# Moving every tile of an HGRN2 and forgetting-attention kernel to a rounder start address in SBUF

## The chip, the cores and the metric

The kernel runs on one core of one Trainium2 chip. A core has TensorE (PE in the profile, its weight loads shown apart as PEld), VectorE (DVE), ScalarE (ACT), GpSimd (POOL) and SyncE (SP, which here only issues DMAs). SBUF is the on-chip working memory; a tile in it is a block of bytes at the same address in each of up to 128 partitions. The metric is the device time of one execution in microseconds.

## The reference, cut to what matters

The program computes two residual layers over 512 tokens of width 2048, all float32. Layer one is a gated linear recurrence (HGRN2) with 16 heads of 128, computed in blocks; layer two is attention with a learned forget gate (FoX), 16 heads of 128, whose keys and values come from the stream after layer one.

```python
def hgrn2_layer(x, norm_w, w_in, lb, out_norm_w, w_out):
    h = rmsnorm(x, norm_w)
    proj = h @ w_in                                  # 2048 -> 8192: q, fz, i, gate
    log_f = jnp.logaddexp(jnp.log(lb), jnp.log1p(-lb) + jax.nn.log_sigmoid(fz))
    k = (1.0 - lb) * jax.nn.sigmoid(-fz)
    o = hgrn2_chunkwise(q, k, i, log_f)
    o = head_rmsnorm(o, out_norm_w) * jax.nn.silu(gate)
    return x + o @ w_out

def fox_layer(x, norm_w, w_in, q_norm_w, out_norm_w, w_out, k, v, F):
    proj = rmsnorm(x, norm_w) @ w_in                 # 2048 -> 4096: q, gate
    q = head_rmsnorm(q, q_norm_w)
    o = forgetting_attention(q, k, v, F)             # softmax(q.k/sqrt(d) + F[t] - F[s])
    o = head_rmsnorm(o, out_norm_w) * jax.nn.silu(gate)
    return x + o @ w_out
```

## The kernel before

**Products.** Each float32 operand is held as two float32r tiles, a rounded value (names ending in h) and the remainder (names ending in l), and a product is three matmuls: h·h, h·l and l·h. `group` computes one 512-column slice of a projection: for each of 16 slices of the 2048 inputs it takes a pair `wh`, `wl` of weights and streams tokens against them. Feature-major groups (L227 to L229) use 128-column pieces of `wh`/`wl` as the stationary operand and stream the 512 columns of `xh`/`xl`; token-major groups (L223 to L225, the value projections) do the reverse, with pieces of `xh`/`xl` stationary and `wh`/`wl` streamed. In the profile an operand list `gm<-xh,wh` names the output, then the streamed operand, then the stationary one.

**Feeding it.** SP loads 512 KB of raw weights into one of two `wr` buffers. ACT casts half of it to `wh` (L432, or L137 where a norm weight is multiplied in) and DVE subtracts to get `wl` (L433, L138).

**Stages.** Stage A runs the projections of layer one, with the recurrence of the heads (`mix_a`) pumped in between; an output product follows, its last three quarters by `quick`, a seven-product scheme on 256-column halves (L282 to L284); stage B and a second output product do the same for layer two, with `mix_b` as the heads' work. `attend` (L426 to L428) is the heads' product with the values, `v_evac` (L413) takes the values out of PSUM, `split` (L432, L433) makes an h and l pair.

**Where tiles lie.** Three pools of SBUF tiles stand one behind another: `cp`, made by `const`, holds small constants, the norm weights, the masks of 32 to 128 bytes and the two score tiles `at`; `sb`, through `nt`, holds what lives all through the program (`xh`, `xl`, `y`, `z`, `wr`, `rstd`); and a pool of the stage, through `mt`, opened anew by `phase`, holds the rest (`wh`, `wl`, `t`, `q`, `k`, `v` and so on). In each pool tiles lie one after another, each size rounded up to 32 bytes. So a constant of 4 bytes or a mask of 96 shifts all that comes behind it, and `rstdc`, 16 bytes at the end of `sb`, shifts the stage's pool by 32 bytes against `sb`. The order of the instructions on each engine is made by a scheduler from the program's dependences.

Of the kernel before, what the change touches and what calls it, by code (L numbers as in the profile page):

```python
# [1 line left out]

# [8 lines left out]
U8 = mybir.dt.uint8  # L11
# [4 lines left out]
P = 128  # L16
# [4 lines left out]
NW = 4  # L21
# [10 lines left out]
def hgrn2_fox(ctx, tc, io):  # L32
# [3 lines left out]
    cp = ctx.enter_context(tc.tile_pool(name="cp", bufs=1))  # L36
    sb = ctx.enter_context(tc.tile_pool(name="sb", bufs=1))
# [4 lines left out]
    uid = [0]  # L42

    def nt(tag, shape, bufs, dt=F32, pool=None):
        uid[0] += 1
        return (pool or sb).tile(list(shape), dt, tag=tag, name=f"{tag}_{uid[0]}", bufs=bufs)

    def const(tag, shape, dt=F32):
        return cp.tile(list(shape), dt, tag=tag, name=tag)

    def view(t, offset, dims):
        return bass.AP(t.tensor, t.offset + offset, [t.ap[0], *dims])
# [7 lines left out]
    def bank():  # L60
        return nt("mx", (P, T), 4, pool=ps)

    def mt(tag, shape, bufs=1, dt=F32):

        return nt(tag, shape, bufs, dt, cur["sb"])
# [36 lines left out]


    eps = const("eps", (P, 1))
    G.memset(eps, EPS)
    ones_f = tmp()
    G.memset(ones_f[:, :P], 1.0)
    ones = const("ones", (P, P), F32R)
    V.tensor_copy(ones, ones_f[:, :P])
    ident = const("ident", (P, P))  # L110
    make_identity(nc, ident)

# [45 lines left out]
    class Chunks:  # L158
# [15 lines left out]
        def load(self):  # L174

            if not self.todo:
                return
            ap, quick, scales, kt = self.todo.pop(0)
            r = nt("wr", (P, 2 * T), 2)
            nc.sync.dma_start(r, ap)  # L180
            if quick:
                self.raw.append((lambda r=r.rearrange("p (a b c) -> p a b c", a=2, c=P): w_split_quick(r, w_sums(r)), 2))
            else:
                for i in range(2):
                    self.raw.append((lambda v=r[:, i * T : (i + 1) * T], k=kt + i: [w_split(v, k, scales)], 1))
# [134 lines left out]
    def sum_parts(x, out_bank):  # L320

        half = P // 2
        s = x
        hl = mt("sl", (P, T), 2, F32R)
        V.tensor_add(s[:half], x[:half], x[half:])
        V.tensor_copy(hl[:half], s[:half])
        V.tensor_sub(hl[half:], s[:half], rd(hl)[:half])
        PE.matmul(out_bank, ones, hl, start=True, stop=True)

    def rsqrt_mean(out, sums, n):  # L330
        S.activation(out, sums, AF.Ln, scale=1.0 / n, bias=eps)
        S.activation(out, out, AF.Exp, scale=-0.5)

    class Norm:
# [15 lines left out]
        def finish(self):  # L350
            b = bank()
            sum_parts(self.acc, b)
            self.row = nt("rstd", (P, T), 1)
            rsqrt_mean(self.row, b, D)
            b2 = bank()
            for w in range(NW):
                PE.transpose(b2[:, w * P : (w + 1) * P], self.row[:, w * P : (w + 1) * P], ident)
            self.col = nt("rstdc", (P, NW, 1), 1)
            V.tensor_copy(self.col, b2.rearrange("p (w c) -> p w c", c=P)[:, :, 0:1])


# [720 lines left out]
```

## Time and profile before

| | us |
|---|---|
| median of 3 runs | 2089.97 |
| lowest, highest run | 2087.96, 2094.06 |
| the profiled execution | 2092.97 |
| its span, first to last instruction | 2091.2 |

The profile page has the busy share of each engine, a strip of 40 slices over the span, the chain of work that ended last, and groups of instructions by source line. A group's row gives the line, engine, operation, out<-in by tile names, shape and count, then its busy time, the mean duration of one in ns, and the idle time of the engine before it with what ended it. Matmuls overlap in the pipeline, and so the duration of one (some 396 ns for 512 columns) is not the time it costs: that is the distance between the starts of two in a row, which the timeline gives.

### The profile page before, as it was taken

To read this page: it belongs to the slowest core of one execution; us is meant where nothing else is said; L and a number is where in the kernel's file an instruction comes from. 1 tells how busy PE (TensorE), PEld (TensorE's weight loads), DVE (VectorE), ACT (ScalarE), POOL (GpSimd) and SP (SyncE) were. 2 spreads that over 40 slices of the span, in tenths; PEclk is the share of its full clock that TensorE was granted. 3 is DMA by queue.
4 is the path that set the end of the run, shared out by engine and by line. 5 is a ranking of instruction groups with operands and counts; after the bars stand their busy time and mean duration, and the time that the engine had idled before them with its cause. 6 is when DMAs were issued, how large, how long until landed. Compare 5 with 4: busy or idle time off the path is not lost.

```text
span 2091.2 us, 28900 instructions
## 1 busy us (share of the span) xinstructions
PE 2028.2 (97%) x10202; PEld 1701.7 (81%) x10202; DVE 1579.0 (76%) x3250; ACT 1132.6 (54%) x2312; POOL 316.1 (15%) x404
## 2 busy tenths in 40 slices
PE   7999999999999999988989999999999999999798
PEld 5888888888888888768977888888888888888698
DVE  8778977988799788769884667665766666685887
ACT  5646655666566465634443555554555556564343
POOL 7303210322132031211210000010001000011100
PEclk9999999999999999989999999999999999999899
DMA  5222222222222222233533232223222222223353
GB/s 172 81 81 81 71 81 71 81 81 71 81 71 81 76 76 71 90 117 117 161 104 91 87 95 91 86 78 99 91 86 87 91 91 86 86 82 109 101 165 108
DMA packets 61408, 195.01 MB, mean 93 GB/s; under 512 B 7872, under 2 KB 8000, under 8 KB 61264
## 3 DMA queue, kind: packets, MB, share of 16 engines
q1 hardware_dynamic: 61120, 193.17, 29.5%
q8 instruction: 80, 1.31, 0.3%
q14 instruction: 64, 0.52, 0.1%
q10 hardware_dynamic: 144, 0.01, 0.0%
HBM read 184.73 MB, written 8.42 MB: 92 GB/s over the span
## 4 chain that ended last, share of the span: by engine, by line
PE 83%; DVE 7%; DMA 3%; ACT 2%; issue 2%; POOL 2%; SPq 0%; DVEq 0%; ACTq 0%; POOLq 0%
PE gm L227 17%; PE gm L229 17%; PE gm L228 17%; PE gm L224 5%; PE gm L223 5%; PE gm L225 5%; DVE wl L433 3%; DMA wr<-in_wb_q 2%; PE mx L580 1%; PE mx L579 1%; PE mx L578 1%; PE mx L427 1%; PE mx L428 1%; PE mx L284 1%; PE mx L426 1%
## 5 line engine op out<-in xcount | busy, mean ns | idle before, releaser
L227 PE MATMUL gm<-xh,wh 128*128 128x512 f32 x1664 | 662.0, 398 | 13.9 <-ACT wh L432 8.3
L228 PE MATMUL gm<-xl,wh 128*128 128x512 f32 x1664 | 661.8, 398 | 0.0
L229 PE MATMUL gm<-xh,wl 128*128 128x512 f32 x1664 | 625.6, 398 | 5.7 <-DVE wl L433 5.5
L227 PEld LDWEIGHTS gm<-xh,wh 128*128 128x128 f32 x1664 | 314.3, 189 | 86.5 <-ACT wh L432 8.3
L229 PEld LDWEIGHTS gm<-xh,wl 128*128 128x128 f32 x1664 | 312.1, 189 | 77.6 <-DVE wl L433 7.0
L228 PEld LDWEIGHTS gm<-xl,wh 128*128 128x128 f32 x1664 | 314.5, 189 | 71.6
L432 ACT CAST wh<-wr 128x512 fp32r<-128x512 f32 (+1 forms) x336 | 217.3, 649 | 232.5 <-PE gm L228 125.8
L433 DVE TENSOR_TENSOR wl<-wr,wh 128x512 fp32r<-128x512 f32 (+1 forms) x336 | 261.8, 783 | 107.7 <-ACT wh L432 101.5
L138 DVE SCALAR_TENSOR_TENSOR wl<-wr,v_b_norm_w,wh 128x256 fp32r<-128x256 f32 (+1 forms) x192 | 113.7, 594 | 152.1 <-ACT wh L137 141.2
L137 ACT ACTIVATE wh<-wr,v_b_norm_w 128x256 fp32r<-128x256 f32 (+1 forms) x192 | 111.9, 586 | 196.8 <-PE gm L228 155.9
L224 PE MATMUL gm<-wl,xh 128*128 128x512 f32 x512 | 203.7, 398 | 0.4 <-DVE wl L433 0.4
L225 PE MATMUL gm<-wh,xl 128*128 128x512 f32 x512 | 202.1, 396 | 0.0
L223 PE MATMUL gm<-wh,xh 128*128 128x512 f32 x512 | 185.8, 396 | 0.0
L137 ACT ACTIVATE wh<-wr,v_kv_norm_w 128x256 fp32r<-128x256 f32 (+1 forms) x192 | 110.3, 575 | 63.2 <-PE gm L225 46.2
L138 DVE SCALAR_TENSOR_TENSOR wl<-wr,v_kv_norm_w,wh 128x256 fp32r<-128x256 f32 (+1 forms) x192 | 111.2, 580 | 38.6 <-ACT wh L137 38.0
L924 POOL TENSOR_SCALAR_AFFINE_SELECT s<-s 128x128 f32<-128x128 f32 x64 | 27.4, 428 | 669.7 <-DVE s L923 669.0
L573 DVE COPY_PREDICATED at<-m,mx 128x128 f32<-128x128 uint8 (+3 forms) x448 | 106.6, 296 | 13.6 <-PE mx L580 13.0
L223 PEld LDWEIGHTS gm<-wh,xh 128*128 128x128 f32 x512 | 95.9, 188 | 22.4 <-DVE q L544 0.2
L224 PEld LDWEIGHTS gm<-wl,xh 128*128 128x128 f32 x512 | 96.2, 188 | 21.5 <-DVE wl L433 0.9
L225 PEld LDWEIGHTS gm<-wh,xl 128*128 128x128 f32 x512 | 96.1, 188 | 20.9
L432 ACT CAST kh<-k 128x512 fp32r<-128x512 f32 (+1 forms) x96 | 56.4, 587 | 52.0 <-PE mx L579 25.8
L382 POOL TENSOR_TENSOR z<-z,t 128x512 f32<-128x512 f32 x32 | 47.9, 1509 | 237.0 <-ACT t L381 236.9
(217 smaller groups left out, 3893.9 us busy)
## 6 DMA issues: line engine op xcount, KB each, us to landing
wr<-in_wa_qf SPq DMA_DIRECT2D x64, 512.0 KB, 3.6
wr<-in_wb_qk SPq DMA_DIRECT2D x64, 512.0 KB, 3.5
wr<-in_wa_v SPq DMA_DIRECT2D x32, 512.0 KB, 3.5
wr<-in_wa_g SPq DMA_DIRECT2D x32, 512.0 KB, 3.5
wr<-in_wb_v SPq DMA_DIRECT2D x32, 512.0 KB, 3.5
wr<-in_wb_g SPq DMA_DIRECT2D x32, 512.0 KB, 3.5
wr<-in_wa_q SPq DMA_DIRECT2D x24, 512.0 KB, 3.6
wr<-in_wb_q SPq DMA_DIRECT2D x24, 512.0 KB, 3.6
```

The source lines that it names most:

```text
L137: S.activation(h[:, c], r[:, c], AF.Copy, scale=w[:, kt : kt + 1])
L138: V.scalar_tensor_tensor(l[:, c], r[:, c], w[:, kt : kt + 1], rd(h)[:, c], op0=ALU.mult, op1=ALU.subtract)
L223: PE.matmul(banks[j], xh, h, start=f, stop=False)
L224: PE.matmul(banks[j], xh, l, start=False, stop=False)
L225: PE.matmul(banks[j], xl, h, start=False, stop=e)
L227: PE.matmul(banks[j], h[:, c], Xh[kt], start=f, stop=False)
L228: PE.matmul(banks[j], h[:, c], Xl[kt], start=False, stop=False)
L229: PE.matmul(banks[j], l[:, c], Xh[kt], start=False, stop=e)
L382: G.tensor_mul(z, z, l)
L432: S.copy(h, src)
L433: return V.tensor_sub(l, src, rd(h))
L573: V.copy_predicated(out, mv, data)
```

## The change

Only start addresses differ. `padded` rounds the bytes of a tile per partition up to a multiple of 64 by allocating a wider tile and handing out its front; `nt` and `const` go through it. And `rstdc` moves from `sb` to `cp`, so that `sb` holds only tiles of 2 KB and of 4 KB. With these roundings `cp` ends at byte 8192, which is four times 2048, where it ended at 7808 before. The instructions, their order on each engine and the semaphores that they wait for are the same in both programs.

```diff
     def nt(tag, shape, bufs, dt=F32, pool=None):
         uid[0] += 1
-        return (pool or sb).tile(list(shape), dt, tag=tag, name=f"{tag}_{uid[0]}", bufs=bufs)
+        return padded(pool or sb, shape, dt, tag, f"{tag}_{uid[0]}", bufs)
+
+    def padded(pool, shape, dt, tag, name, bufs=1):
+
+        n = math.prod(shape[1:])
+        unit = 64 if dt == U8 else 16
+        if n % unit == 0:
+            return pool.tile(list(shape), dt, tag=tag, name=name, bufs=bufs)
+        t = pool.tile([shape[0], -(-n // unit) * unit], dt, tag=tag, name=name, bufs=bufs)[:, :n]
+        return t.rearrange("p (a b) -> p a b", b=shape[2]) if len(shape) == 3 else t
 
     def const(tag, shape, dt=F32):
-        return cp.tile(list(shape), dt, tag=tag, name=tag)
+        return padded(cp, shape, dt, tag, tag)
...
-            self.col = nt("rstdc", (P, NW, 1), 1)
+            self.col = nt("rstdc", (P, NW, 1), 1, pool=cp)
```

Start addresses of the tiles in the two built programs, as the remainder by 2048 and by 64. A is the stage of layer one, B that of layer two.

| tiles | before, mod 2048 (mod 64) | after, mod 2048 (mod 64) |
|---|---|---|
| `xh`, `xl`, `y`, `z`, `wr`, `rstd` | 1664 (0) | 0 (0) |
| `wh`, `wl` in A | 1696 (32) | 0 (0) |
| `wh`, `wl` in B | 672 (32) | 1024 (0) |
| `wm`, `tm`, `th` and `t`, `q`, `k`, `g` in A | 1696 (32) | 0 (0) |
| `kh`, `kl` in A | 1184 (32) | 1536 (0) |
| `ah`, `al` in A | 224, 1248 (32) | 704, 1728 (0) |
| `v`, `vh`, `vl` in A | 224 (32) | 704 (0) |
| `v`, `vh`, `vl` in B | 960 (0) | 1600 (0) |
| `fb`, `s` in B | 672 (32) | 1024 (0) |

More of the change, by code (lines that the diff above doesn't have):

```diff
@@ L1 @@
+import math
 from contextlib import ExitStack
```

## The prediction

> **What bounds the kernel now.** I read first the page: busy shares, the clock strip, the chain of waits by engine. It tells which engine's speed the end depends on.
>
> ```profile
> span 2091.2 us, 28900 instructions
> PE 2028.2 (97%) x10202; PEld 1701.7 (81%) x10202; DVE 1579.0 (76%) x3250; ACT 1132.6 (54%) x2312; POOL 316.1 (15%) x404
> PEclk9999999999999999989999999999999999999899
> PE 83%; DVE 7%; DMA 3%; ACT 2%; issue 2%; POOL 2%; SPq 0%; DVEq 0%; ACTq 0%; POOLq 0%
> ```
>
> TensorE holds 83% of the chain at a clock that is never withheld for long. The rest is DVE 7%, DMA 3%, ACT and POOL 2% each. Second, the table by stage, since 97% is an average: stage A, the first output product's `quick` part, stage B, and the last product.
>
> ```profile
> 65.00:900.00 835.00, 829.90 (x3996) 689.78 (x3995) 700.84 (x1666) 504.68 (x1107) 179.07 (x237) 1.00 0.26 80
> 955.00:1065.00 110.00, 101.94 (x810) 99.47 (x811) 96.99 (x142) 51.24 (x67) 24.18 (x12) 0.97 0.43 135
> 1160.00:1940.00 780.00, 779.77 (x3553) 636.51 (x3552) 511.23 (x1011) 428.67 (x909) 52.04 (x81) 1.00 0.29 90
> 1940.00:2092.00 152.00, 130.81 (x1012) 125.93 (x1010) 126.65 (x205) 55.06 (x68) 7.57 (x7) 0.95 0.38 125
> ```
>
> Columns: the stretch and its length, then busy time of PE, PEld, DVE, ACT and POOL, the granted clock, the DMA share. In A and B, 1615 us together, PE waits 5.3 us in all. There nothing but the pace of matmuls counts, and a saving on DVE, ACT or POOL is worth nothing. In the two output products (262 us) PE waits 29.3 us, and the feeding engines share the chain.
>
> So a change of addresses can act in two ways: by the pace of a matmul in A and B, or by the durations of DVE, ACT, POOL and DMA in the output products. Third, therefore, the pace: the timeline of PE where a token-major group (first three rows) meets a feature-major one. Columns: start, duration, instruction.
>
> ```profile
> 661.23 0.40 PE L225 MATMUL gm<-wh,xl 128*128 128x512 f32 x1
> 661.47 0.39 PE L224 MATMUL gm<-wl,xh 128*128 128x512 f32 x1
> 661.70 0.39 PE L225 MATMUL gm<-wh,xl 128*128 128x512 f32 x1
> 661.93 0.40 PE L227 MATMUL gm<-xh,wh 128*128 128x512 f32 x1
> 662.16 0.40 PE L228 MATMUL gm<-xl,wh 128*128 128x512 f32 x1
> 662.39 0.40 PE L229 MATMUL gm<-xh,wl 128*128 128x512 f32 x1
> ```
>
> Starts lie 0.23 us apart, which is what a 512-column matmul costs; 0.40 is its passage through the pipeline.
>
> **The change, term by term.** No instruction is added, removed or moved, so every term is a count times a possible change of duration. The trace of before helps because its tiles lie both ways: by the addresses in the table above, `xh`, `y`, `z`, `wr` already start on multiples of 64, while most tiles of a stage start 32 bytes past one.
>
> *Matmul, streamed operand at 32 against 0 mod 64.* The first three rows above stream `wh` or `wl` (32 past), the last three `xh` or `xl` (on a multiple). Both have the pace 0.23 us. The groups by form, stage A alone:
>
> ```profile
> L227 PE MATMUL gm<-xh,wh 128*128 128x512 f32 x738 | 292.4, 396 | 0.9 <-ACT v L413 0.9
> L227 PEld LDWEIGHTS gm<-xh,wh 128*128 128x128 f32 x738 | 138.8, 188 | 31.8 <-ACT v L413 1.3 <-DVE z L378 0.2
> L224 PE MATMUL gm<-wl,xh 128*128 128x512 f32 x253 | 100.4, 397 | 0.4 <-DVE wl L433 0.4
> L223 PEld LDWEIGHTS gm<-wh,xh 128*128 128x128 f32 x252 | 47.2, 188 | 10.9 <-DVE q L544 0.2
> L427 PE MATMUL mx<-al,vh 128*128 128x384 f32 x16 | 5.4, 339 | 0.0
> L426 PE MATMUL mx<-ah,vh 128*128 128x384 f32 x16 | 5.4, 337 | 0.0
> ```
>
> 396 ns streaming the aligned `xh`, 397 streaming `wl`. A weight load takes 188 ns whether it reads `wh` (32 past) or `xh` (aligned), and it hides under a pace of 230 in any case. Term: 0.
>
> *Matmul, a streamed row that crosses a multiple of 2 KB.* 512 float32 columns are 2048 bytes; before, each such row crosses one multiple of 2 KB, after, rows of `xh` and `xl`, and of A's `wh` and `wl`, cross none. The trace has no 512-column matmul of the second sort. The nearest are the last two rows: in `attend` the 384 columns of `ah` lie at 224 to 1760 within their 2 KB, those of `al` at 1248 to 2784, across a multiple. 337 against 339 ns: 2 ns at most, as large as the rows' other scatter. Bounds: 0 and 2 ns. Matmuls concerned: 26 feature-major groups (24 projections and the first group of each output product) stream `xh`/`xl` 16 x 4 x 3 = 192 times each, 4 token-major groups of A `wh`/`wl` as often: 30 x 192 = 5760, nearly all in the stretches where PE never waits. So 0 to -11.5 us. I take 0, because 2 ns is hardly more than the scatter of rows that all cross one (396 and 397 above).
>
> *Distance of the two streams that PE reads.* In A the starts of `xh` and `wh` are 32 bytes apart mod 2048, in B 992; after, 0 in A and 1024 in B. The groups by form of stage B:
>
> ```profile
> L227 PE MATMUL gm<-xh,wh 128*128 128x512 f32 x768 | 304.1, 396 | 0.0
> L227 PEld LDWEIGHTS gm<-xh,wh 128*128 128x128 f32 x768 | 144.3, 188 | 33.9
> L224 PE MATMUL gm<-wl,xh 128*128 128x512 f32 x220 | 87.9, 399 | 0.0
> ```
>
> 396 and 188 as in A; L224 399 against 397. Distance costs nothing that the rows show. Bounds: 2 ns a matmul either way, value 0.
>
> *DVE and ACT.* `v`, `vh` and `vl` all start 32 past a multiple of 64 in A and all on one in B, with the same instructions. The tile `v`, stage A, then stage B (min/median/max ns):
>
> ```profile
> L413 ACT ACTIVATE v<-gm,rstdc x64: 349/414/488, 112.2 to 665.1; 128x128 f32<-128x128 f32 x64
> L432 ACT CAST vh<-v x16: 619/621/757, 118.6 to 794.5; 128x512 fp32r<-128x512 f32 x16
> L433 DVE TENSOR_TENSOR vl<-v,vh x16: 678/691/694, 121.4 to 795.1; 128x512 fp32r<-128x512 f32 x16
> ...
> L413 ACT ACTIVATE v<-gm,rstdc x64: 342/402/474, 1180.4 to 1743.7; 128x128 f32<-128x128 f32 x64
> L432 ACT CAST vh<-v x16: 619/621/753, 1185.9 to 1851.3; 128x512 fp32r<-128x512 f32 x16
> L433 DVE TENSOR_TENSOR vl<-v,vh x16: 681/692/1787, 1186.8 to 1853.3; 128x512 fp32r<-128x512 f32 x16
> ```
>
> The cast has the median 621 both times, the subtraction 691 and 692. Only L413 is shorter when aligned, 402 against 414; 64 x 12 ns = 0.8 us of ACT, in a stage where PE does not wait. It would show only as ACT time: 0 at the end, -0.8 at most. And a three-operand subtraction whose operands all share one remainder (1664), `xl` of `y` and `xh`:
>
> ```profile
> L433 DVE TENSOR_TENSOR xl<-y,xh x48: 674/680/1776, 835.8 to 1914.4; 128x512 fp32r<-128x512 f32 x48
> ```
>
> Median 680: equal remainders mod 2048 don't slow DVE. Term for both engines: 0. If all 7% of the chain that are DVE's (146 us) followed the 680 against 691, it would be 1.6%, or 2.4 us, either way.
>
> *POOL.* The groups of two adds of one size, first with all operands aligned, then with all 32 past:
>
> ```profile
> L347 POOL TENSOR_TENSOR rstd<-rstd,z 128x512 f32<-128x512 f32 x30 | 52.1, 1738 | 104.6 <-ACT z L346 103.7
> L561 POOL TENSOR_TENSOR g<-t,t 128x512 f32<-128x512 f32 x16 | 27.7, 1728 | 264.1 <-ACT t L556 258.7 <-DVE t L557 5.4
> ```
>
> 1738 against 1728, no gain in it: 0; 10 ns of 1738 on POOL's 2% of the chain (42 us) would be 0.2 us.
>
> *DMA.* `wr` starts at 1664, half-way between two multiples of 256, and at a multiple of 2048 after. The list of DMA issues, KB each and median us to landing:
>
> ```profile
> z<-in_x SPq DMA_DIRECT2D x16, 256.0 KB, 3.0
> fb<-fd SPq DMA_DIRECT2D x16, 256.0 KB, 3.2
> z<-x1d SPq DMA_DIRECT2D x16, 256.0 KB, 3.6
> wr<-in_wa_q SPq DMA_DIRECT2D x24, 512.0 KB, 3.6
> wr<-in_wb_o SPq DMA_DIRECT2D x8, 512.0 KB, 3.5
> ```
>
> Into `z` (a multiple of 64) 256 KB take 3.0 or 3.6 us, into `fb` (32 past one) 3.2: no order by address. Two `wr` rows at one address differ by 0.1 of 3.6. The chain has 3% of DMA, 63 us or 18 loads of 3.5 us; 0.1 each is 1.8 us. Bounds -1.8 and +1.8, value 0.
>
> The Trainium skill, "DMA: Bandwidth & Descriptors", section "How a descriptor splits into AXI transactions", says that a descriptor which does not begin on a multiple of 256 B starts at the boundary below and pays for bytes that it doesn't use. For a row of 4096 bytes begun 128 past a boundary that makes 132 beats of 32 B in place of 128, if it holds for the end that is written; by it the 63 us would shrink by 3%, an estimated 1.9 us. No run here shows it, and the rows above speak neither for nor against so small a share.
>
> **Sum.** All terms are 0; the profiled execution took 2092.97 us (span 2091.2 and 1.8 around it) and the changed kernel would take the same again. It stands 3.0 us above the median of the three runs, so the forecast for the median is 2089.97 + 0 = 2090.0 us. By the skill's rule on descriptors it would be 2088.1.
>
> **Rivals.** What a measurement of this kernel can tell from no change is about 0.3%, 6.3 us; it lies at 2083.7 and 2096.3.
>
> *A row within one 2 KB block streams faster.* Mechanism and count as above: 5760 matmuls, PE-bound. For it: the 2 ns between `al` and `ah`, and that no aligned 512-column row has been seen. Against it: a scatter of the same size where addresses play no such part, 397 against 399 for L224 in the two stages. At 2 ns: 2090.0 - 11.5 = 2078.5 us. It decides from 1.1 ns on (6.3 us / 5760), half a percent of the pace.
>
> *Equal remainders make streams collide (slower).* In A after, `xh` that is streamed and `wh` that is loaded begin at the same remainder, where 32 bytes lay between. If the load's reads held up the stream, each of the 17 x 192 = 3264 matmuls of stage A and its output group would pay. For it: L224 is 2 ns apart between stages. Against it: `xl<-y,xh` at equal remainders is as fast as any, and the load of 188 ns has 42 ns to spare. At 4 ns, twice the scatter of the rows: 2090.0 + 13.1 = 2103 us; at 2 ns 2096.5. It decides from 1.9 ns.
>
> *The loads into `wr` land sooner.* -1.8 us in the output products, 2088.2: below what can be told.
>
> *The change doesn't do what it says.* Were a wait or an order different, the terms would not be the whole; the two programs have the same order and waits, so this has almost no weight.
>
> **Chances.** Forecast (nothing that can be told) 0.71, sooner loads 0.05, faster streaming 0.14, collision 0.08, something unnamed 0.02, split evenly. Faster 0.15, same 0.76, slower 0.09. The likeliest case's own range is 2085 to 2095, the spread of the three runs a little widened. The range for 8 in 10 goes down to the faster streaming at 2 ns and up to the edge of the collision: 2079 to 2097.
>
> **What would show it.** In the changed profile: PE starts 0.23 us apart as before; L227 and L224 at 396 to 399 ns, loads at 188; the medians of `vl<-v,vh` near 691, of `vh<-v` at 621 in both stages; PE waiting as long in the output products (29 us); `wr` landing in 3.5 to 3.6. The forecast is wrong if the pace in A or B moves by more than 1 ns, which shows as A's 835 us or B's 780 us growing or shrinking by over 3 us; if the stages stay and the output products move, it is DVE or DMA.

## The result, and the profile after

The changed kernel takes 2066.59 us in the median of 4 runs (2064.19 to 2067.86); the kernel before, run beside it, 2090.59 (2087.96 to 2094.06, also 4). The ratio is 0.9883, 95% interval 0.9865 to 0.9901: 24 us, or 1.2%, faster. The prediction said 2090.0 and a range of 2079 to 2097; the time lies below the range.

The page of the profile after: span, busy shares, and the chain of waits by engine.

```profile
span 2066.1 us, 28900 instructions
PE 1997.4 (97%) x10202; PEld 1702.9 (82%) x10202; DVE 1581.7 (77%) x3250; ACT 1130.6 (55%) x2312; POOL 318.9 (15%) x404
PE 77%; DVE 13%; ACT 3%; issue 3%; POOL 2%; DMA 2%; DVEq 0%; SPq 0%; ACTq 0%; POOLq 0%
```

The counts are those of before, and DVE, ACT and POOL are busy as long as before to within 3 us. Only PE's line differs: 1997.4 us in place of 2028.2, 31 us less for the same 10202 matmuls. Of them 24 to 25 us reach the end, and the chain shifts from PE (83% to 77%) to DVE (7% to 13%).

The stages, in the prediction's stretches. Columns: stretch and length, busy time of PE, PEld, DVE, ACT, POOL with their counts, granted clock, DMA share, GB/s.

```profile
65.00:900.00 835.00, 825.69 (x4026) 696.22 (x4025) 703.05 (x1668) 504.21 (x1109) 179.62 (x237) 1.00 0.26 81
955.00:1065.00 110.00, 103.80 (x824) 101.24 (x824) 100.68 (x146) 51.18 (x69) 21.10 (x10) 0.98 0.44 142
1160.00:1940.00 780.00, 770.67 (x3592) 643.09 (x3590) 528.03 (x1037) 432.50 (x912) 55.48 (x82) 0.99 0.30 93
```

In A's 835 us PE now starts 4026 matmuls and not 3996; B ends inside its stretch. Since the stretches no longer hold the same work, stretches that hold the same number of PE instructions are better. First the kernel before, inside A and inside B:

```profile
75.00:880.00 805.00, 801.26 (x3874) 667.05 (x3873) 677.84 (x1638) 485.16 (x1074) 169.24 (x230) 1.00 0.25 78
1190.00:1880.00 690.00, 689.77 (x3148) 563.22 (x3147) 459.43 (x919) 381.00 (x807) 41.63 (x70) 1.00 0.29 89
```

Then the kernel after:

```profile
73.60:872.00 798.40, 790.75 (x3873) 667.63 (x3872) 678.93 (x1637) 483.57 (x1073) 169.84 (x231) 1.00 0.26 79
1180.00:1856.00 676.00, 675.46 (x3149) 563.21 (x3148) 459.46 (x919) 381.01 (x807) 41.96 (x70) 1.00 0.29 90
```

The same work takes 6.6 us less in A (805.0 to 798.4) and 14.0 less in B (690.0 to 676.0). The granted clock is the same, and PEld, DVE and ACT are busy the same time to 0.4%. So the matmul's own pace has changed, and it shows at once where a stretch without other work is read from end to end. The timeline of PE at the same place of stage B, in each case the 25 feature-major matmuls in a row ahead of a head's product of keys and queries (`mx<-kh,qh`); start, duration, instruction. Before:

```profile
1249.43 0.40 PE L227 MATMUL gm<-xh,wh 128*128 128x512 f32 x1
...
1255.03 0.40 PE L227 MATMUL gm<-xh,wh 128*128 128x512 f32 x1
```

After (line numbers are higher by 10 in this kernel):

```profile
1237.74 0.39 PE L237 MATMUL gm<-xh,wh 128*128 128x512 f32 x1
...
1243.18 0.39 PE L237 MATMUL gm<-xh,wh 128*128 128x512 f32 x1
```

24 distances take 5.60 us before and 5.44 after: 233.3 ns against 226.7, 2.8%. Two neighbouring starts can't show this, since they are written to 0.01 us. Nor can the mean duration show its size, which holds the passage through the pipeline; the groups by form of after, stage A:

```profile
L237 PE MATMUL gm<-xh,wh 128*128 128x512 f32 x720 | 282.4, 392 | 1.1 <-ACT v L423 0.9 <-DVE z L388 0.2
L234 PE MATMUL gm<-wl,xh 128*128 128x512 f32 x251 | 98.6, 393 | 0.4 <-DVE wl L443 0.4
```

396 has become 392 and 397 has become 393, while the pace fell by 6 ns. From here on "pace" is the mean distance between starts of neighbouring matmuls of one kind.

**Where 24 us come from and where more was lost.** I added up the distances between consecutive starts of PE in both traces, with what goes beyond a matmul's longest ordinary distance (245 ns for 512 columns) counted as a wait. The rows of the 512-column groups leave out the last matmuls of the output products' groups, which `all PE` has. Microseconds, before to after:

| part | pace | waits |
|---|---|---|
| A, 512-column groups (3171) | 740.8 to 725.5 | 17.4 to 23.2 |
| A, the heads' matmuls (1029) | 132.1 to 132.3 | 1.1 to 2.9 |
| B, 512-column groups (3220) | 751.6 to 733.5 | 5.3 to 5.7 |
| B, the heads' matmuls | 91.1 to 91.1 | 2.4 to 2.4 |
| `quick` (2016 of 256 columns) | 240.1 to 242.6 | 69.0 to 68.1 |
| all PE | 1987.6 to 1956.0 | 95.3 to 102.4 |

The 512-column groups, with those of the output products, give 34 us. `quick` gives 2.5 back by a slower pace, and stage A gives 7.6 back in waits. Sum: 31.6 less pace, 7.1 more waits, 24.5 us. Some 8.5 us of A's waits, before, lie in the first 65 us of the program. What the others are, the waits of PE in the stretch 65 to 900 show (waiting tile and line, releaser; total us, times, longest). Before:

```profile
PE mx L578 <- ACT mh L432: 2.4, 4, 1.0
PE gm L229 <- DVE wl L433: 1.4, 1, 1.4
PE gm L227 <- ACT v L413: 0.9, 1, 0.9
```

After:

```profile
PE mx L588 <- ACT mh L442: 4.9, 4, 1.6
PE gm L239 <- DVE wl L443: 1.7, 1, 1.7
PE gm L237 <- ACT v L423: 0.9, 1, 0.9
PE mx L437 <- DVE al L443: 0.5, 1, 0.5
```

A faster PE comes to the heads' products with `mh` (an operand that ACT casts at the end of a chain over POOL and DVE) before that chain is done, and waits 1.2 us each time where it waited 0.6 before: 2.5 us of the 7.6. The waits for one `wl` and one `v` stand in both kernels. Another 1.4 us are no waits for data: eight matmuls right behind the longest wait for `mh`, with starts 0.43 us apart, in the stretch of lower clock that the last section shows. The rest is spread over many shorter waits.

### The profile page after: what moved, and what is told of

Read it like the earlier page. It is cut to its first block, busy times and chain, and to the rows that moved or that the text cites. A ratio compares the mean times of both kernels' runs of the same rounds, so it can differ in the third digit from the quotient of the medians.

```text
span 2066.1 us, 28900 instructions
## 1 busy us (share of the span) xinstructions
PE 1997.4 (97%) x10202; PEld 1702.9 (82%) x10202; DVE 1581.7 (77%) x3250; ACT 1130.6 (55%) x2312; POOL 318.9 (15%) x404
## 4 chain that ended last, share of the span: by engine, by line
PE 77%; DVE 13%; ACT 3%; issue 3%; POOL 2%; DMA 2%; DVEq 0%; SPq 0%; ACTq 0%; POOLq 0%
PE gm L239 16%; PE gm L237 16%; PE gm L238 16%; PE gm L234 5%; PE gm L233 5%; PE gm L235 5%; DVE wl L443 3%; PE mx L294 1%; PE mx L292 1%; PE mx L293 1%; DMA wr<-in_wa_q 1%; PE mx L590 1%; PE mx L588 1%; PE mx L589 1%; DVE ml L443 1%
## 5 line engine op out<-in xcount | busy, mean ns | idle before, releaser
L237 PE MATMUL gm<-xh,wh 128*128 128x512 f32 x1664 | 653.5, 393 | 13.6 <-ACT wh L442 7.8
L238 PE MATMUL gm<-xl,wh 128*128 128x512 f32 x1664 | 653.3, 393 | 0.0
L239 PE MATMUL gm<-xh,wl 128*128 128x512 f32 x1664 | 617.7, 393 | 7.1 <-DVE wl L443 6.5
```

The costliest lines, as they stand in the source:

```text
L237: PE.matmul(banks[j], h[:, c], Xh[kt], start=f, stop=False)
L238: PE.matmul(banks[j], h[:, c], Xl[kt], start=False, stop=False)
L239: PE.matmul(banks[j], l[:, c], Xh[kt], start=False, stop=e)
```

## The experiments

The theory that I formed from the addresses: the pace depends on where the streamed operand begins relative to the operand whose columns are loaded as weights. Before, `xh` and `wh` are 32 bytes apart; after, 0 (A) or 1024 (B). The rivals: each operand's own alignment (to 64, to 2 KB, or a row that crosses a multiple of 2 KB), or less contention from DVE, ACT and DMA, whose tiles were moved too.

### A kernel of matmuls alone, by start addresses

```diff
+    mv = cp.tile([P, 4 * T], F32R, tag="mv", name="mv")
+    st = cp.tile([P, 4 * T], F32R, tag="st", name="st")
...
+    for i in range(48): PE.matmul(out(i), w(i, 0), a(i, 0), start=i % 3 == 0, stop=i % 3 == 2)
+    for i in range(48): PE.matmul(out(i), w(i, 32), a(i, 0), start=i % 3 == 0, stop=i % 3 == 2)
+    for i in range(48): PE.matmul(out(i), w(i, 64), a(i, 0), start=i % 3 == 0, stop=i % 3 == 2)
...
+    for i in range(48): PE.matmul(out(i), w(i, 1696), a(i, 1664), start=i % 3 == 0, stop=i % 3 == 2)
```

`a(i, m)` streams 512 columns that begin m bytes into a 2 KB piece of the tile `mv`, `w(i, s)` loads 128 columns that begin s bytes into a 512-byte piece of `st`. Nothing of the reference is computed. The expectation below takes m and s for remainders by 2 KB. They are not quite: in the built program 1152 bytes lie ahead of the pool, then 768 and 2048 of two other tiles, so that `mv` starts at 3968, which is 128 bytes below a multiple of 2 KB, and so does `st`, 8192 bytes on. Distances and remainders by 64 and 128 are as m and s say; a row begins on a multiple of 2 KB for m = 128.

> This kernel leaves out the whole computation: it holds only float32r matmuls of 512 columns (a few of 256), three to a bank as in the projections, in blocks of 48, with the streamed operand starting m bytes and the stationary one s bytes past a multiple of 2 KB, m and s from 0 to 1664, and nothing else on the chip's engines meanwhile. The changed kernel's 512-column matmuls start 227 ns apart, those of before 233. Theory 64 (either operand off a multiple of 64 costs): 227 where m and s are both multiples of 64, 233 elsewhere. Theory block (the streamed operand has to start on a multiple of some larger power of two up to 1024, the stationary one is free): 227 for m = 0, 1024 and perhaps 512 or 256, 233 for the others, whatever s. Theory distance (what counts is how far the two operands that TensorE reads lie apart): 227 for m = s and for distances of 512, 233 for m and s 32 apart. Theory others (TensorE's reads collide with those of DVE, ACT or DMA): one pace for all blocks here.

Mean distance of starts in a block of 48, without the first two, in ns, by m of the streamed operand (rows) and s of the weights (columns):

| streamed | 0 | 32 | 64 | 128 | 192 |
|---|---|---|---|---|---|
| 0 | 226.7 | 233.4 | 233.4 | 232.5 | 228.9 |
| 32 | 233.4 | 227.2 | 233.4 | 234.4 | 233.2 |
| 64 | 228.9 | 233.3 | 226.7 | 233.4 | 232.5 |

And m and s set to the remainders of the kernels' tiles, so that the distances are the kernels' own: 1664 with 1696 (A before) 233.4, 1664 with 672 (B before) 233.4; reversed, for token-major groups, 233.4 and 233.3; 0 with 0 (A after) 226.7; 0 with 1024 (B after) 227.4 and 1024 with 0 226.7. Two rows alike in nothing but the distance mod 256: 1664 with 128 (6 x 256 = 1536 apart) takes 226.9, 672 with 1184 (512 apart) 227.4.

So the fast pace stands on the diagonal, and a multiple of 256 bytes counts as 0. The own alignment counts for nothing: 32 with 32 is as fast as 0 with 0, and 64 with 0 is not. A row that crosses a multiple of 2 KB is as fast as one that doesn't: 128 with 128, the only pair on the diagonal whose rows cross none, takes 226.9. A block needs some matmuls to settle: behind the block (0, 32), the first seven distances of (32, 32) run from 225 to 236 ns, and all later ones inside the block are 226 or 227. The order of the groups shows even in the mean durations, though flattened; lines 95 and 96 are the pairs of A and B before, L42 is (0, 32), streamed operand first, L53 (64, 0), L48 (32, 32), L41 (0, 0), L102 and L104 are 256 columns wide with (0, 0) and (1664, 1696):

```profile
L95 PE MATMUL bk<-mv,st 128*128 128x512 f32 x48 | 11.4, 396 | 0.0
L96 PE MATMUL bk<-mv,st 128*128 128x512 f32 x48 | 11.4, 396 | 0.0
L42 PE MATMUL bk<-mv,st 128*128 128x512 f32 x48 | 11.4, 395 | 0.0
L53 PE MATMUL bk<-mv,st 128*128 128x512 f32 x48 | 11.1, 391 | 0.0
L48 PE MATMUL bk<-mv,st 128*128 128x512 f32 x48 | 11.1, 390 | 0.0
L41 PE MATMUL bk<-mv,st 128*128 128x512 f32 x48 | 11.1, 389 | 0.0
L102 PE MATMUL bk<-mv,st 128*128 128x256 f32 x48 | 5.9, 283 | 0.0
L104 PE MATMUL bk<-mv,st 128*128 128x256 f32 x48 | 5.8, 281 | 0.0
```

The last two rows turn the sign: 256 columns take 120.0 ns at distance 0 and 118.2 with the stream 32 bytes behind the weights, as `xh` and `wh` of `quick` lay before. That fits `quick` becoming slower.

The Trainium skill, "SBUF — State Buffer", section "Who interferes with whom", gives PE two read ports, one for the moving operand and one for LDWEIGHTS, and calls them independent. By that one would expect no effect of one operand's place on the other's reads. The measurement differs in this: with neither operand's own place mattering, the distance between the two moves the pace from 227 to 233 ns. Whether the ports are where this happens is not shown.

### The same with DVE, ACT and DMA at work

```diff
+        nc.sync.dma_start(wr[k // 4 % 2], io["w"][k // 4 % 8])
+        S.copy(wh[k % 2], r)
+        V.tensor_sub(wl[k % 2], r, wh[k % 2].bitcast(F32))
```

> The same matmuls, again without the rest of the computation, with one cast on ACT, one subtraction on DVE (2 KB tiles) for every three matmuls and a 512 KB load for every twelve running beside them on tiles of their own. Theories 64, block and distance: as in the run without the other engines. Theory others: the paces part here, 227 where TensorE's operands and the tiles of the others have one remainder, 233 elsewhere.

A stretch of 200 us, with PE never idle, shows DVE busy for 152, ACT for 140 and the DMA engines for 47%:

```profile
100.00:300.00 200.00, 200.00 (x867) 162.61 (x866) 152.22 (x236) 140.11 (x236) 0.00 (x0) 1.00 0.47 155
```

The paces are those of the quiet kernel to 0.1 ns: 226.7 for (0, 0), 233.4 for A before. Contention with DVE, ACT and DMA is out, as cause of the 6.6 ns and as part of it. POOL does nothing in this run; it does nothing in the quiet kernel either, which has both paces.

### The whole kernel with everything moved by 64 bytes

```diff
-            self.col = nt("rstdc", (P, NW, 1), 1, pool=cp)
+            self.col = cp.tile([P, 32], F32, tag="rstdc", name=f"rstdc_{uid[0]}", bufs=1)[:, :NW].rearrange("p (a b) -> p a b", b=1)
```

> The changed kernel with the one tile in front of all 2 KB tiles wider by 64 bytes: every tile from there on starts 64 bytes later, so all are on multiples of 64, none on one of 128, and no distance between two tiles changes. Theory 64 and theory distance: 2066 us as the changed kernel, pace 227. Theory block: 2090 us as before, pace 233.

2065.85 us (2065.26 to 2066.73), ratio to before 0.9871 (0.9855 to 0.9888), as fast as after. The paces are 227.9 ns feature-major and 228.4 token-major. Beginning on a multiple of 2 KB is worth nothing; every 512-column row crosses one here.

### The changed kernel with the stage's pool 32 bytes further

```diff
-        if n % unit == 0:
+        if n % unit == 0 or n > T:
...
-        Xl[kt] = nt(f"xl{kt}", (P, T), 1, F32R)
+        Xl[kt] = nt(f"xl{kt}", (P, T + (8 if kt == KT - 1 else 0)), 1, F32R)[:, :T]
```

> The changed kernel with 32 bytes between the pool that lives all through and the pool of the stage: xh, xl, y, z, wr stay on multiples of 2 KB, the tiles of a stage (wh, wl and the rest) start 32 past a multiple of 64, as before the change. Theory 64 and theory distance: 2090 us, pace 233 in feature-major and token-major groups alike. Theory block: feature-major groups, which stream xh and xl, keep 227, token-major ones, which stream wh and wl, go to 233: 8 of 34 groups, 2072 us.

2091.94 us (2089.94 to 2094.2), ratio 0.9997 (0.9987 to 1.0006). With `xh` still on a multiple of 2 KB, 32 bytes between it and `wh` undo the whole gain; the paces are 233.3 and 233.4. Together with the run before, this rules out the theory of larger blocks in the kernel itself. Alignment to 64 and distance expect the same of both runs; the next two tell them apart.

### Only `rstdc` moved, nothing padded

```diff
-            self.col = nt("rstdc", (P, NW, 1), 1)
+            self.col = nt("rstdc", (P, NW, 1), 1, pool=cp)
```

> The kernel before with one line of the change: rstdc in the constants' pool, no padding. The 2 KB tiles of both pools then start 32 past a multiple of 64 (remainder 1696 of 2048, and 672 in stage B), so no operand of the projections is on a multiple of 64, but streamed and stationary ones are a multiple of 256 apart. Theory distance: 2066 us, pace 227. Theory 64: 2090 us, pace 233.

2066.24 us (2066.03 to 2067.45), ratio 0.9879 (0.9865 to 0.9894). This one line against the kernel before gives all of the gain: `rstdc` held 32 bytes behind the 2 KB tiles of `sb`, so every tile of the stage's pool lay 32 bytes off. Here `xh`, `wh` and nearly all else begin 32 bytes past a multiple of 64, distance 0. The groups by form, stage A:

```profile
L227 PE MATMUL gm<-xh,wh 128*128 128x512 f32 x724 | 283.4, 392 | 1.1 <-ACT v L413 0.9 <-DVE z L378 0.2
L224 PE MATMUL gm<-wl,xh 128*128 128x512 f32 x252 | 98.9, 393 | 0.4 <-DVE wl L433 0.4
```

392 and 393 as after, with none of the multiples of 64.

### Only the padding, `rstdc` left where it was

```diff
-            self.col = nt("rstdc", (P, NW, 1), 1, pool=cp)
+            self.col = nt("rstdc", (P, NW, 1), 1)
```

> The change without that line: all small tiles padded to multiples of 64, rstdc left in the pool that lives all through. xh and xl then start at remainder 1984, wh and wl at 0 or 1024: all on multiples of 64, 64 apart. Theory 64: 2066 us, pace 227. Theory distance: feature-major groups stream 64 bytes behind their weights, distance 192 of 256, pace 233 as before; token-major ones 64 ahead, pace 229: 1536 matmuls x 4.5 ns = 6.9 us less, of which the changed kernel kept some 0.7, so about 2086 us.

2088.28 us (2085.08 to 2090.9), ratio 0.9987 (0.9977 to 0.9996) to a before of 2092.1. All tiles are on multiples of 64 here, 64 bytes apart. Feature-major groups, weights 64 past the stream, have 233.5 ns; token-major ones, the stream 64 past, 229.7, as in the table of the small kernel (0 with 64: 233.4, 64 with 0: 228.9). `quick` is at 117.0. I expected 2086; at 3.6 ns, the 8 x 192 token-major matmuls give 5.5 us and `quick` 2016 x 1.5 = 3.0, of which 3.8 arrived by the medians, 0.8 to 4.8 by the interval of the ratio. Groups by form, stage A:

```profile
L237 PE MATMUL gm<-xh,wh 128*128 128x512 f32 x716 | 283.5, 396 | 0.9 <-ACT v L423 0.9
```

### Finer distances and other widths

```diff
+    for i in range(48): PE.matmul(out(i), w(i, 0), a(i, 4), start=i % 3 == 0, stop=i % 3 == 2)
...
+    for i in range(48): PE.matmul(out(i)[:, :256], w(i, 0), a(i, 32, 256), start=i % 3 == 0, stop=i % 3 == 2)
...
+    for i in range(48): PE.matmul(out(i), w(i, i % 2 * 64), a(i, i % 2 * 64), start=i % 3 == 0, stop=i % 3 == 2)
+    for i in range(48): PE.matmul(out(i), w(i, i % 2 * 64), a(i, 64 - i % 2 * 64), start=i % 3 == 0, stop=i % 3 == 2)
```

> Matmuls alone once more, the rest of the computation left out; the stationary operand at 0, the streamed one d bytes past it, d in finer steps for 512 columns, and in steps of 32 for 128, 192, 256, 320 and 384 columns; then blocks in which the two operands' starts alternate by 64 or 128 bytes from matmul to matmul, either so that a matmul's own two operands agree, or so that the streamed operand agrees with the weights of the next matmul, which are loaded while it streams. Theory distance, own operands: 227 in the first kind, about 231 (the mean of 229 and 233) at 64 and 232.5 at 128 in the second. Theory distance, next load: the reverse. Theory 64 is out by the first sweep (227 with both at 32, 233 with 0 and 64) and would give 227 in all of these. For 256 columns distance 0 gave 120 and 224 gave 118: a distance with less than 117 would be a use for the output products.

| streamed minus weights, bytes | 0 | 4 | 16 | 32 | 64 | 96 | 128 | 160 | 192 | 252 |
|---|---|---|---|---|---|---|---|---|---|---|
| 512 columns, ns | 226.7 | 238.2 | 231.6 | 233.4 | 228.9 | 233.3 | 232.4 | 234.0 | 233.4 | 231.1 |
| 256 columns, ns | 119.8 | | | 117.8 | 117.8 | 119.8 | 118.7 | 118.7 | 117.8 | |

(32, 64, 128 and 192 of the first row are from the first kernel.) 320 columns take 146.5 to 146.7, 192 columns 111.7 and 128 columns 111.6 at each distance tried; 384 columns 173.3 to 176.7. So the effect is neither a step at 64 nor one sign for all widths.

The last blocks were to tell which pair counts. If each matmul's operands agree and the next one's lie 64 off, the pace is 231.8; if the stream agrees with the weights of its neighbour instead, 233.2. With 128: 228.3 and 230.0. Neither comes to 227. A fifth block, weights at 0 and the stream in turn at 0 and 64, has the distances 0 and 64 with its own weights and with the next ones alike; both readings would give 228, the mean of 226.7 and 228.9, and it takes 231.1. So a pace per distance holds only while all matmuls of a row share the distance, and alternation costs something of its own. Since the next weights load while a row streams, the neighbour's could have been what counts; that the own pair does better speaks against it, but neither is shown. That stays open.

### Distance 64 in `quick`

Both kernels run on one chip, the first of them the changed kernel once more.

> The changed kernel once more, as the neighbour of the next run on one chip: 2066 us, 512-column pace 227, 256-column pace 119.8 in the output products.

```diff
-        m = mt("tm", (P, 4, TN), 1)
+        m = mt("tm", (P, 4 * TN + 16), 1)[:, : 4 * TN].rearrange("p (a b) -> p a b", b=TN)
```

> The changed kernel with the tile tm, the first of the pool of an output product, wider by 64 bytes: th, tl, wh and wl of quick start 64 past a multiple of 256, xh and xl on one, as in the run with padding alone, whose 256-column matmuls had 117.0; stages A and B keep distance 0. Theory distance: 256-column pace 117.0 in place of 119.8, 2.8 ns x 2016 = 5.6 us less of matmul pace in stages that already wait 68 us for their feed; if all reaches the end 2061, if two thirds 2062.5 us. Rival: in those stages the feed sets the end, and the time stays at 2066.

The changed kernel: 2065.12 us (2064.5 to 2065.63), ratio 0.987 (0.9854 to 0.9887). With `th`, `tl`, `wh` and `wl` of `quick` 64 bytes further: 2065.26 (2064.8 to 2065.81), ratio 0.9872 (0.9857 to 0.9887). No difference. The pace in `quick` did fall, from 119.8 to 117.0 ns, and all of PE's pace from 1956.0 to 1951.0 us. This is no mean of the table: only the four of seven products that stream `xh` and `xl` change their distance, `th` moves along with `wh` and keeps 0, yet its products went from 119.8 to 117.5. But PE's waits rose from 100.3 to 104.0. A stretch of 110 us in the first output product, the changed kernel and then the other:

```profile
930.00:1040.00 110.00, 102.80 (x802) 99.21 (x801) 100.09 (x147) 48.95 (x64) 24.45 (x14) 0.97 0.42 135
```

```profile
930.00:1040.00 110.00, 100.97 (x801) 97.26 (x801) 99.22 (x147) 48.85 (x63) 23.95 (x14) 0.97 0.41 133
```

The same 801 or 802 matmuls, PE busy 1.8 us less, and not one more of them done. So PE's pace doesn't set the end there; that the feed does is argued from DVE being busy for 100 of the 110 us. No version faster than the changed kernel was found.

## Why the prediction was wrong

**Distance of the two streams that PE reads.** This term failed, and it carries the whole miss. The prediction compared A (32 apart) with B (992 apart), found 396 ns in both, and concluded "Distance costs nothing that the rows show". But 992 is 4 x 256 - 32: by the measure that counts, A and B are the same case, 32 bytes apart, and both are slow (233.4 each in the small kernel). So the comparison could not show an effect. The value 0, bounds 2 ns either way, measured -6.6 ns in the undisturbed stretch (233.3 to 226.7) and, over all matmuls of the groups, 233.4 to 227.8 (feature-major) and 233.3 to 228.3 (token-major). 26 x 192 x 5.6 + 8 x 192 x 5.0 = 36 us by these means; 34 us were found in the trace.

**The bounds.** They came from the scatter of mean durations, 396 to 399 ns. Durations show 4 ns where the pace moved by 5.6, and the prediction never took the pace itself to better than 0.01 us. Even with the distance seen as untested, the bound could not be 2 ns: no projection of before had distance 0. The heads' products had (`ah` and `vh` in A both start at 224), the 384-column rows of the prediction among them, but they come in threes between others, and a long row at one distance was not there to read.

**Streamed operand at 32 against 0 mod 64.** That the own alignment costs nothing was right (32 with 32: 227.2, 0 with 0: 226.7). The evidence was sound for that and no more, since `wh` streamed against `xh` and `xh` against `wh` are 32 and -32 apart, both slow.

**A row within one 2 KB block streams faster (rival).** Sign, engine and stages as it happened, but by luck: its mechanism fell. With everything 64 further, or 32, each row crosses a multiple of 2 KB and the kernel is as fast. Its 2 ns would have given 2078.5 and were 5 to 6.

**Equal remainders make streams collide (rival).** The right pair of addresses with the sign reversed: at 512 columns equal remainders are the fastest place. At 256 columns they are indeed slower, by 2 ns, and `quick` lost 2.5 us.

**DVE, ACT, POOL, DMA.** The values of 0 held for the end, two readings behind them did not. The tile `v` of after, stage A then stage B (min/median/max ns):

```profile
L423 ACT ACTIVATE v<-gm,rstdc x64: 351/414/480, 110.2 to 658.5; 128x128 f32<-128x128 f32 x64
L442 ACT CAST vh<-v x16: 621/622/767, 116.6 to 787.9; 128x512 fp32r<-128x512 f32 x16
L443 DVE TENSOR_TENSOR vl<-v,vh x16: 680/692/700, 119.4 to 788.5; 128x512 fp32r<-128x512 f32 x16
...
L423 ACT ACTIVATE v<-gm,rstdc x64: 348/406/472, 1170.2 to 1721.8; 128x128 f32<-128x128 f32 x64
L442 ACT CAST vh<-v x16: 607/620/755, 1175.7 to 1827.1; 128x512 fp32r<-128x512 f32 x16
L443 DVE TENSOR_TENSOR vl<-v,vh x16: 680/692/1782, 1176.6 to 1829.2; 128x512 fp32r<-128x512 f32 x16
```

622 and 692 in A, with `v` now on a multiple of 64, where 621 and 691 stood. The taking out of `v`, which the prediction called shorter when aligned, stays at 414 in A with `v` aligned: its 402 in B was not the alignment's doing. The loads of weights and of `z`, in the list of DMA issues of after:

```profile
wr<-in_wa_q SPq DMA_DIRECT2D x24, 512.0 KB, 3.5
z<-in_x SPq DMA_DIRECT2D x16, 256.0 KB, 3.0
fb<-fd SPq DMA_DIRECT2D x16, 256.0 KB, 3.2
wr<-in_wb_o SPq DMA_DIRECT2D x8, 512.0 KB, 3.5
```

3.5 where 3.6 and 3.5 stood. The trace has the landings to the nanosecond: the median of all 320 loads into `wr` is 3.544 us before and 3.503 after. So they do land sooner on a multiple of 256, but by 0.04 us, or 1.2%; for the 18 loads of the prediction's chain that is 0.7 us. The prediction's estimate from the Trainium skill, "DMA: Bandwidth & Descriptors", section "How a descriptor splits into AXI transactions", was 3%.

**What bounds the kernel.** Right: A and B are PE-bound, so a change of pace came through: by the table of pace and waits 17.7 of 18.1 us in B. A passed on less, 7.5 of 15, in part since its heads' chains over ACT, POOL and DVE were only just ahead of PE. What would show the forecast wrong came as it was named: the same work of A and of B took 6.6 and 14.0 us less, and both are over 3.

## What to carry to other kernels

A reading that finds no effect between two cases is worth nothing until one knows that they differ in what matters: list the differences between addresses modulo several powers of two, not the addresses, and ask whether the case after the change occurs in the trace at all. Measure the pace of a pipelined engine over a long undisturbed row of starts, and not by mean durations. For 512-column float32r products in a PE-bound kernel, place the streamed operand and the weights a multiple of 256 bytes apart (a 32-byte tile between the two pools cost 1.2% here), and count on only part of the gain where other engines are just ahead.

## What the runs showed of the hardware

- The pace of 512-column float32r matmuls depends on (start of stream minus start of weights) mod 256: 227 ns at 0, 229 at 64, 231 to 235 at most other distances tried, 237 to 238 at 240 and 4. This holds for rows of matmuls that share one distance; in alternating rows the paces don't follow from it. Why is not shown; the runs only say that neither address alone matters and that DVE, ACT and DMA have no part in it.
- The sign depends on the width: at 256 columns distance 0 is among the slowest (120 against 117.8 at 32, 64 and 192), at 320 columns and at 192 and below there is no effect.
- The median 512 KB load into `wr`, with rows of 4096 bytes, lands in 3.503 us where `wr` starts on a multiple of 256 (after), 3.544 at 128 past one (before), 3.556 at 64 (all moved by 64), 3.577 at 160 (only `rstdc` moved) and 3.611 at 192 (only the padding); other executions with `wr` on a multiple have 3.516 to 3.522.
- In the profiled execution of after, PE waited 1.6 us of 3 and was then granted a clock of 0.60 for 4 us. Columns as in the stage tables:

```profile
761.00:764.00 3.00, 1.40 (x7) 0.86 (x7) 3.00 (x8) 2.06 (x7) 1.37 (x4) 0.97 0.14 16
764.00:768.00 4.00, 4.00 (x13) 3.11 (x12) 4.00 (x12) 0.48 (x2) 0.00 (x0) 0.60 0.34 125
768.00:772.00 4.00, 4.00 (x24) 3.47 (x23) 4.00 (x16) 2.06 (x6) 0.00 (x0) 1.00 0.00 0
```

13 matmuls where the next 4 us hold 24. Another execution of the same program, with the same waits of 4.9 and 1.7 us in stage A, has no such stretch there, so a wait of that length doesn't always bring it.
